# Slots and banks by one assignment, and a search that goes on from kept states, in a two-layer hybrid decoder trunk

## The chip, the cores and the metric

The kernel runs on one core of one Trainium2 chip. A core has TensorE (PE: matmuls into PSUM, a memory of eight banks), VectorE (DVE), ScalarE (ACT), GpSimd (POOL) and SyncE (SP), whose queue here issues every DMA transfer. The engines run side by side, each through its own list of instructions in the order in which they stand in it, and wait for one another on semaphores. The metric is the time of one launch in microseconds; shorter is better.

## The reference

Two layers over 1024 tokens of width 1024. Each layer normalizes, makes one projection, gives its columns to four token mixers, normalizes each mixer's output, projects back and adds; then comes a SwiGLU FFN of width 2816.

```python
for l in range(DEPTH):
    h = rmsnorm(x, attn_norm[l])
    proj = h @ w_in[l]
    (c_q, c_kv, k_r, g_b, g_c, u_conv, u_pool, q_sw, k_sw, v_sw) = jnp.split(proj, pts, axis=-1)
    y_a = mla_attention(...)        # 4 heads, causal, latent keys and values
    y_b = short_gated_conv(...)     # causal, width 3
    y_c = multiscale_pool(...)      # trailing means over 2, 4, 8, 16 tokens
    y_d = swa_sink_attention(...)   # window 128, grouped keys, ALiBi, sinks
    ...                             # RMSNorm of each group, then side by side as `mixed`
    x = x + mixed @ w_o[l]
    h2 = rmsnorm(x, ffn_norm[l])
    gate, up = jnp.split(h2 @ w_gate_up[l], 2, axis=-1)
    x = x + (jax.nn.silu(gate) * up) @ w_down[l]
return rmsnorm(x, final_norm)
```

## The kernel before

**The work.** Activations lie transposed, channels on the 128 partitions and tokens along the row, in two halves of 512 tokens. Every fp32 operand is split into a high part in the type fp32r (a copy that casts: line 301, or 223 for weights, on ScalarE) and the rest as a low part (a subtraction: line 304, or 224 for weights, on VectorE). A product is three fp32r matmuls: high by high, high by low, low by high (`mm3`, line 281). So TensorE cannot start on an operand before ScalarE has cast it, and cannot do its third matmul before VectorE has made the low part. In each layer the program first writes the projections and the four mixers (attention scores at lines 999 to 1001, transposes of probabilities at 1053, their products with the values at 1065), then the output projection, then the FFN, whose matmuls follow a scheme that forms seven products of sums of blocks (L1184 and L1186 make sums of the normalized input blocks, L1271 loads sums of weights that were made earlier and stored in DRAM under the name `gd`, L1459 is the SiLU on ScalarE, which needs a table load of its own, L1236 and L1238 load gate and up weights).

**Storage.** SBUF operands live in 47 slots of 128 x 2 x 512 floats, each one pair of halves (`Slots`; tiles are named u, then the slot, then a running number: `u33_4418` is tile 4418 in slot 33). PSUM tiles (ps_mm, ps_s, ps_t, ps_pv) get one of eight banks. A tile may be written once all readers of the slot's or bank's earlier tile are done; the semaphores for that follow from the choice of slot.

**The order.** No order is written by hand. `scheduled_kernel` traces the program once, builds a graph of the instructions with their dependencies and a cost for each (`Order`), and simulates the engines with ready lists (`_forward`), each engine taking the ready instruction with the lowest rank. In five rounds it gives banks (`Order.banks`) and slots (`Slots.place`, from the spans of `Order.spans`) by the planned begin and end of every tile, traces again, and runs a short search; the best round gets a long one (`_search`). A trial of the search changes ranks, either of instructions within a random stretch or along the chain that ends in one idle gap of TensorE, and replans the whole program; it is kept if the mean of four simulations with random lateness of the DMAs (`lates`) is lower. The order found is then imposed on each engine's list, SyncE's queue of DMAs included. In the numbers below, L281 of TensorE stands for all products, since the helper records their line.

Of the kernel before, what the change touches and what calls it, by code (L numbers as in the profile page):

```python
# [6 lines left out]

# [49 lines left out]
class Slots:  # L57

    def __init__(self, pool, n, spans=None):
        self.pool = pool
        self.spans = spans
        self.made = []
        self.until = [0.0] * n
        self.places = deque(range(n))
        self.halves = {F32: deque(), F32R: deque()}
        self.cur = [None] * n
        self.dt = [None] * n

    def place(self):

        if self.spans is None:
            return self.places.popleft()
        start, end = self.spans[len(self.made)]
        i = max(self.places, key=lambda i: u if (u := self.until[i]) <= start else -u)
        self.places.remove(i)
        self.until[i] = end
        return i

    def pair(self, dt):
        i = self.place()
        self.cur[i] = self.pool.tile([P, 2, HT], dt, name=f"u{i}", tag=f"u{i}", bufs=1)
        self.made.append(self.cur[i].name)
        self.dt[i] = dt
        return 2 * i
# [9 lines left out]
    def free(self, i):  # L96
        h = self.halves[self.dt[i // 2]]
        if i ^ 1 in h:
            h.remove(i ^ 1)
            self.places.append(i // 2)  # L100
        else:
            h.append(i)

    def free_pair(self, i):
        self.places.append(i // 2)
# [25 lines left out]
def trunk_kernel(ctx: ExitStack, tc: tile.TileContext, ins, out, given=None, spans=None, made=None):  # L131
# [10 lines left out]
    slots = Slots(ctx.enter_context(tc.tile_pool(name="slots", bufs=1)), N_U, spans)  # L142
    if made is not None:
        made.append(slots.made)
# [1663 lines left out]
TRIALS = 1500 if numba else 40  # L1808
# [42 lines left out]
def _forward(eng, kind, seen, taken, kb, want, late, hop, start, to, sync, count, rank, fixed, order):  # L1851

    n = eng.size
    left = count.copy()
    ready = np.zeros(n)
    end = np.zeros(n)
    begin = np.zeros(n)
    free = np.zeros(5)
    lk, lv = np.zeros((5, n)), np.zeros((5, n), np.int64)
    nk, nv = np.zeros((5, n)), np.zeros((5, n), np.int64)  # L1860
    ln, nn = np.zeros(5, np.int64), np.zeros(5, np.int64)
    done = np.zeros(5, np.int64)
    flying = np.zeros(LANES)
    issued = 0
    served = 0.0
    lock = 0.0
    table = 0
    for k in range(n):
        if left[k] == 0:
            e = eng[k]  # L1870
            _push(lk[e], lv[e], ln[e], 0.0, k)
            ln[e] += 1
    for _ in range(n):
        best, b = 1e18, -1
        for e in range(5):
            if fixed:
                if done[e] == 0:
                    pass
                i = done[e]
                k = order[e, i] if i < order.shape[1] else -1  # L1880
                if k < 0 or left[k] > 0:
                    continue
                t = max(free[e], ready[k])
            else:
                while ln[e] > 0 and lk[e, 0] <= free[e]:
                    k = lv[e, 0]
                    _drop(lk[e], lv[e], ln[e])
                    ln[e] -= 1
                    _push(nk[e], nv[e], nn[e], rank[k], k)
                    nn[e] += 1  # L1890
                if nn[e] > 0:
                    t = free[e]
                elif ln[e] > 0:
                    t = lk[e, 0]
                else:
                    continue
            if e == SP and issued >= LANES:
                t = max(t, flying[issued % LANES])
            if t < best:
                best, b = t, e  # L1900
        if b < 0:
            return end, begin, False
        t, e = best, b
        if fixed:
            k = order[e, done[e]]
        else:
            while ln[e] > 0 and lk[e, 0] <= t:
                k = lv[e, 0]
                _drop(lk[e], lv[e], ln[e])
                ln[e] -= 1  # L1910
                _push(nk[e], nv[e], nn[e], rank[k], k)
                nn[e] += 1
            k = nv[e, 0]
            _drop(nk[e], nv[e], nn[e])
            nn[e] -= 1
            order[e, done[e]] = k
        done[e] += 1
        more = 0.0
        if kind[k] >= TWO:
            get = max(t + 0.08, lock)  # L1920
            more = get - t - 0.08
            lock = get + max(0.05, seen[k] - (0.16 if kind[k] == TWO else 0.19))
        elif e == ACT and want[k] >= 0:
            if want[k] != table:
                more = 0.0 if kind[k] == TABLE else 1.29
                table = want[k]
        begin[k] = t
        free[e] = t + taken[k] + more
        end[k] = t + seen[k] + more
        if e == SP:  # L1930
            served = max(t + (1.31 if kind[k] == LOAD else 0.41), served) + kb[k] / 322.0
            end[k] = served + 0.82 + late[k]
            flying[issued % LANES] = end[k]
            issued += 1
        for i in range(start[k], start[k + 1]):
# [5 lines left out]
            if left[j] == 0 and not fixed:  # L1941
                _push(lk[eng[j]], lv[eng[j]], ln[eng[j]], ready[j], j)
                ln[eng[j]] += 1
    return end, begin, True
# [51 lines left out]
def _trials(arrays, graph, lates, order, limit):  # L1996

    eng, kind, seen, taken, kb, want, hop = arrays
    start, to, sync, count = graph[:4]
    none = np.zeros(0)  # L2000
    total = 0.0
    for s in range(lates.shape[0]):
        end, _, ok = _forward(
            eng, kind, seen, taken, kb, want, lates[s], hop, start, to, sync, count, none, True, order
        )
        if not ok:
            return 1e18
        total += end.max()
        if total + (lates.shape[0] - 1 - s) * (limit - 2.0) > lates.shape[0] * limit:
            return 1e18  # L2010
    return total / lates.shape[0]
# [3 lines left out]
def _search(arrays, graph, lates, margin, rank, trials, seed):  # L2015
# [5 lines left out]
    width = 0  # L2021
    for e in range(5):
        width = max(width, (eng == e).sum())
    order = -np.ones((5, width), np.int64)
    end, begin, _ = _forward(
        eng, kind, seen, taken, kb, want, margin, hop, start, to, sync, count, rank, False, order
    )
    best = _trials(arrays, graph, lates, order, 1e9)
    first = best
    wins = 0  # L2030
    rank = begin
    trial = -np.ones((5, width), np.int64)
    before = -np.ones(n, np.int64)
    for it in range(trials):
        new = rank.copy()
        if it % 2:
            lo = np.random.random() * end.max()
            hi = lo + math.exp(np.random.random() * 3.5 + 0.7)
            s = math.exp(np.random.random() * 4.0 - 1.5)
            some = np.random.randint(0, 10)  # L2040
            for k in range(n):
                if lo <= begin[k] < hi and (some >= 5 or eng[k] == some):
                    new[k] += s * np.random.randn()
        else:
            last = -1
            gaps = 0.0
            for q in range(width):
                k = order[PE, q]
                if k < 0:
                    break  # L2050
                if last >= 0:
                    gap = begin[k] - begin[last] - taken[last]
                    if gap > 0.04:
                        gaps += gap
                last = k
            pick = np.random.random() * gaps
            last, k = -1, -1
            for q in range(width):
                k = order[PE, q]
                if last >= 0:  # L2060
                    gap = begin[k] - begin[last] - taken[last]
                    if gap > 0.04:
                        pick -= gap
                        if pick <= 0:
                            break
                last = k
            for e in range(5):
                last = -1
                for q in range(width):
                    j = order[e, q]  # L2070
                    if j < 0:
                        break
                    before[j] = last
                    last = j
            s = math.exp(np.random.random() * 4.5 - 1.5)
            for _ in range(np.random.randint(3, 40)):
                new[k] -= s
                p, t = before[k], -1.0
                if p >= 0:
                    t = begin[p] + taken[p]  # L2080
                for i in range(bstart[k], bstart[k + 1]):
                    j = bto[i]
                    r = end[j] + hop[eng[k]] if bsync[i] else begin[j]
                    if r > t:
                        p, t = j, r
# [3 lines left out]
        e1, b1, _ = _forward(  # L2089
            eng, kind, seen, taken, kb, want, margin, hop, start, to, sync, count, new, False, trial  # L2090
        )
        if e1.max() > end.max() + 1.5:
            continue
        got = _trials(arrays, graph, lates, trial, best)
        if got < best:
            best = got
            rank, end, begin = b1, e1, b1
            order, trial = trial, order
# [384 lines left out]
```

## Time and profile before

| | |
|---|---|
| median of three runs | 2044.93 us (2044.12 to 2046.39) |
| the profiled execution | 2045.38 us |
| its span, first to last instruction | 2043.6 us |
| mean granted TensorE clock | 0.997 |
| TensorE without work in the span | 20.7 us (2043.6 - 2022.9) |
| DMA | 308.13 MB, mean 151 GB/s |

A row of the timeline gives the start, the length, the engine, the line, the operation, what it writes and reads, the shapes, how many were merged, and in brackets how long the engine had been idle and who ended that. A matmul's record of 512 columns lasts about 0.39 us, though the next one starts 0.227 us later; so starts, not lengths, tell the pace. A row by stretches gives for each engine the busy time and in brackets the number of instructions.

### The profile page before, as it was taken

How to read it: one execution, taken by the hardware profiler on the slowest of the kernel's cores; microseconds unless marked ns; L12 is line 12 of the kernel's file. 1: busy time of each engine (PE TensorE's matmuls, PEld its weight loads, DVE VectorE, ACT ScalarE, POOL GpSimd, SP SyncE). 2: the span in 40 equal slices, each digit the busy share in tenths (PEclk: the TensorE clock that was granted, in tenths of full speed). 3: DMA queues.
4: the chain of work that ended last, by engine and by line, in shares of the span. 5: the costliest groups of instructions: out<-in, count | busy, mean ns of one | idle time of the engine just before them, and what ended most of it. 6: DMA issues, size and time to landing. Idle time of an engine off the chain costs nothing. (4 is left out here: it accounts for less than half of the span.)

```text
span 2043.6 us, 26485 instructions
## 1 busy us (share of the span) xinstructions
PE 2022.9 (99%) x9398; PEld 1672.6 (82%) x9398; DVE 1578.5 (77%) x2553; ACT 998.8 (49%) x1753; POOL 438.9 (21%) x340
## 2 busy tenths in 40 slices
PE   9999999999999999999999999999999999999998
PEld 7888788878888888888888878888788888888887
DVE  8989979998677777655657999799977777776555
ACT  7458657743333334444434576577433333354342
POOL 0300000025565661000003000000356556500000
PEclk9999999999999999999999999999999999999999
DMA  6310223435555556766513112243455555487542
GB/s 244 127 44 21 84 63 110 149 128 179 179 177 183 176 188 246 259 211 222 176 38 128 56 27 78 65 134 119 145 191 186 177 173 191 169 296 235 195 161 98
DMA packets 144133, 308.13 MB, mean 151 GB/s; under 512 B 14080, under 2 KB 61184, under 8 KB 144000
## 3 DMA queue, kind: packets, MB, share of 16 engines
q1 hardware_dynamic: 144000, 306.43, 44.4%
q8 instruction: 74, 1.21, 0.2%
q14 instruction: 59, 0.48, 0.1%
HBM read 215.67 MB, written 89.65 MB: 149 GB/s over the span
## 5 line engine op out<-in xcount | busy, mean ns | idle before, releaser
L281 PE MATMUL ps_mm<-u,u 128*128 128x512 f32 (+1 forms) x3374 | 843.5, 390 | 7.0 <-ACT u L301 2.8
L281 PEld LDWEIGHTS ps_mm<-u,u 128*128 128x128 f32 x3374 | 615.4, 189 | 129.7 <-ACT u L301 3.6
L281 PE MATMUL ps_s<-u,u 128*128 128x512 f32 x2724 | 652.0, 389 | 0.2 <-DVE u L1214 0.2
L281 PEld LDWEIGHTS ps_s<-u,u 128*128 128x128 f32 x2724 | 510.9, 188 | 108.1 <-DVE u L1214 0.6
L301 ACT CAST u<-u 128x1024 fp32r<-128x1024 f32 (+2 forms) x426 | 361.8, 868 | 478.0 <-PE ps_s L281 116.3
L304 DVE TENSOR_TENSOR u<-u,u 128x1024 fp32r<-128x1024 f32 (+2 forms) x426 | 461.3, 1100 | 154.7 <-ACT u L301 107.0
L281 PE MATMUL ps_t<-u,u 128*128 128x512 f32 (+1 forms) x1092 | 251.9, 377 | 0.0
L281 PEld LDWEIGHTS ps_t<-u,u 128*128 128x128 f32 x1092 | 196.1, 188 | 39.1 <-DVE te L380 0.5
L281 PE MATMUL ps_pv<-u,u 128*128 128x512 f32 x696 | 167.4, 389 | 0.0
L281 PEld LDWEIGHTS ps_pv<-u,u 128*128 128x128 f32 x696 | 130.6, 188 | 27.3 <-DVE tp L1670 0.3
L1277 POOL TENSOR_TENSOR u<-u 128x512 f32<-128x512 f32 x38 | 73.3, 1928 | 226.9 <-DVE u L304 174.2
L1459 ACT ACTIVATE tp<-tp 128x512 f32<-128x512 f32 x76 | 48.0, 632 | 129.3 <-DVE tp L380 129.3
L1062 POOL MEMSET u<- 128x128 f32 x32 | 6.0, 214 | 471.9 <-PE ps_mm L281 250.9
L1247 POOL TENSOR_TENSOR u<-u,u 128x512 f32<-128x512 f32 x38 | 55.6, 1464 | 205.5 <-PE ps_s L281 109.2
L770 POOL TENSOR_TENSOR u<-u,u 128x512 f32<-128x512 f32 x6 | 8.0, 1337 | 413.1 <-ACT sm L628 326.4
L301 ACT CAST u<-ps_t 128x512 fp32r<-128x512 f32 (+3 forms) x132 | 64.8, 502 | 41.3 <-PE ps_t L643 16.6
L1539 POOL TENSOR_TENSOR u<-u 128x352 f32<-128x352 f32 x64 | 79.5, 1244 | 22.4 <-DMA u<-in_w_dn 18.7
L304 DVE TENSOR_TENSOR u<-ps_t,u 128x512 fp32r<-128x512 f32 (+3 forms) x132 | 75.2, 580 | 11.4 <-ACT u L301 10.7
L306 ACT ACTIVATE u<-u,par 128x512 fp32r<-128x512 f32 x92 | 64.6, 719 | 30.7 <-DVE u L380 10.3
L1461 DVE TENSOR_TENSOR tp<-tp,u 128x512 f32<-128x512 f32 x76 | 66.4, 873 | 16.3 <-ACT tp L1459 16.2
L345 ACT ACTIVATE tn<-u 128x512 f32<-128x512 f32 (+1 forms) x91 | 52.6, 597 | 52.2 <-DVE u L1723 45.4
L1249 POOL TENSOR_TENSOR u<-u,u 128x512 f32<-128x512 f32 x38 | 71.8, 1890 | 1.6
(199 smaller groups left out, 2383.5 us busy)
## 6 DMA issues: line engine op xcount, KB each, us to landing
u<-in_w_gu SPq DMA_DIRECT2D x94, 512.0 KB, 4.0
ad<-u SPq DMA_DIRECT2D x154, 256.0 KB, 2.1
u<-ad SPq DMA_DIRECT2D x70, 512.0 KB, 6.0
u<-in_w_dn SPq DMA_DIRECT2D x64, 352.0 KB, 3.3
qd<-u SPq DMA_DIRECT2D x64, 352.0 KB, 2.8
u<-qd SPq DMA_DIRECT2D x32, 512.0 KB, 5.2
u<-in_w_in SPq DMA_DIRECT2D x28, 512.0 KB, 3.9
u<-in_w_dn SPq DMA_DIRECT2D x24, 512.0 KB, 6.5
```

What stands on the lines that cost most here:

```text
L281: pe.matmul(o, w, r, start=start and k == 0 and i == 0, stop=stop and k == n - 1 and i == 2, skip_group_check=again,)
L301: a = act.copy(hi, f)
L304: dve.tensor_tensor(out=lo, in0=f, in1=rd(hi), op=ALU.subtract)
L306: a = act.activation(hi, f, AF.Copy, scale=gain)
L345: act.activation(q, f, AF.Square)
L770: pool.tensor_tensor(out=F.ap(q + 1), in0=a21, in1=a22, op=ALU.add)
L1247: pool.tensor_tensor(out=F.ap(q + 1), in0=a21, in1=a22, op=ALU.add)
L1249: pool.tensor_tensor(out=a21, in0=F.ap(q + 1), in1=a11, op=ALU.add)
L1277: pool.tensor_tensor(out=q4, in0=q4, in1=F.ap(self.raw[1] + 1), op=ALU.add)
L1459: last_silu = act.activation(g, g, AF.Silu)
L1461: dve.tensor_tensor(out=g, in0=g, in1=r, op=ALU.mult)
L1539: pool.tensor_tensor(out=o, in0=a, in1=b, op=ALU.add)
```

## The change

It replaces three pieces of the planner; no instruction of the trunk is added or removed.

- Slots and banks. Before, a tile took, in the program's order, the place that had been free for the shortest time at its planned start (or, with none free, the one that gets free first). Now all tiles are chained at once by a linear assignment over the whole plan: following one tile by another in the same place costs 1/(gap + 0.5) for a planned gap, and 10 and more for an overlap.
- The search. It keeps the state of the simulation at 60 moments of the accepted plan. A trial begins from the last kept state ahead of its change, runs to 60 us behind the changed stretch, and is dropped there if TensorE has then not worked at least 0.02 us more than in the accepted plan. There are 40000 trials instead of 1500, and both kinds of trial now pick their place by a gap of TensorE.
- The four simulations that judge a trial now also shake ACT, DVE and POOL instructions, by an exponential of mean 0.03 us less that mean.

```diff
     def place(self):
-        if self.spans is None:
+        if self.homes is None:
             return self.places.popleft()
-        start, end = self.spans[len(self.made)]
-        i = max(self.places, key=lambda i: u if (u := self.until[i]) <= start else -u)
+        i = self.homes[len(self.made)]
         self.places.remove(i)
-        self.until[i] = end
         return i
...
-TRIALS = 1500 if numba else 40
+TRIALS = 40000 if numba else 40
+STOPS, HORIZON = 60, 60.0
...
+@compiled
+def _worked(arrays, s, t):
+
+    taken, begin, order, m = arrays[3], s[3], s[8], s[6][10]
+    w = 0.0
+    for i in range(m):
+        k = order[PE, i]
+        if begin[k] >= t:
+            break
+        w += min(taken[k], t - begin[k])
+    return w
...
-            lo = np.random.random() * end.max()
-            hi = lo + math.exp(np.random.random() * 3.5 + 0.7)
...
+        k = at[min(m - 1, np.searchsorted(gaps[:m], np.random.random() * total))]
+        new = rank.copy()
+        hi = s[3][k]
+        lo = hi
+        if it % 2:
+            lo = max(0.0, hi - math.exp(np.random.random() * 4.0))
+            hi = lo + math.exp(np.random.random() * 3.5 + 0.7)
...
+        _copy(marks[max(0, min(STOPS - 1, int((lo - 1.0) / step)))], work)
...
+        stop = hi + HORIZON
+        _run(arrays, graph, margin, new, False, stop, work)
+        if _worked(arrays, work, stop) < _worked(arrays, s, stop) + 0.02:
             continue
-        got = _trials(arrays, graph, lates, trial, best)
+        _run(arrays, graph, margin, new, False, 1e18, work)
+        if work[2].max() > s[2].max() + 1.5:
+            continue
+        got = _trials(arrays, graph, lates, work[8], best)
...
-        self.lates = np.stack([moves * draw.exponential(0.5, self.n) for _ in range(4)])
+        others = np.array([e in ("Activation", "DVE", "Pool") for e in self.engine])
+        self.width = max(self.engine.count(e) for e in self.ENGINES)
+        self.lates = np.stack(
+            [
+                draw.exponential(moves * 0.5 + others * 0.03, self.n) - others * 0.03
+                for _ in range(4)
+            ]
+        )
...
+    @staticmethod
+    def chains(start, over, born, gone, places):
+
+        n = len(start)
+        gap = start[None, :] - over[:, None]
+        cost = np.where(gap > 0, 1.0 / (np.maximum(gap, 0) + 0.5), 10.0 - 10.0 * np.minimum(gap, 0))
+        cost[gone[:, None] >= born[None, :]] = 1e7
+        full = np.zeros((n + places, n + places))
+        full[:n, :n] = cost
+        after = [int(k) for k in linear_sum_assignment(full)[1]]
+        home, i = [None] * n, 0
+        for k in sorted(set(range(n)).difference(after[:n])):
+            while k < n:
+                home[k] = i
+                k = after[k]
+            i += 1
+        return home
...
     def banks(self, begin, end):
...
-            b = max(range(8), key=lambda b: free[b] if free[b] <= start else -free[b])
-            free[b] = max(end[k] for k in self.users[m])
-            given.append(b)
-        return given
...
+        return self.chains(start, over, born, gone, 8)
```

What it does to the lists is shown at three places. The new program's line numbers are higher by 4 for the trunk (L301 is L305). Names have the slot's number after u.

ScalarE at the entry to the FFN of layer 0. `_4420` is the high part of the first FFN weights, cast from `_4418`; the rows on `tp_` cast sums of input blocks; `_4158` is a gate block that SiLU works on. Before:

```order
L301 CAST u43_4327<-u22_4321 128x512
L301 CAST u14_4385<-tp_4379 128x512
L301 CAST u25_4391<-tp_4388 128x512
L301 CAST u44_4395<-tp_4389 128x512
L1459 ACT_TABLE_LOAD
L1459 ACTIVATE u1_4158<-u1_4158 128x512
L301 CAST u5_4420<-u33_4418 128x1024
L301 CAST u31_4405<-tp_4399 128x512
```

And in the new program:

```order
L305 CAST u13_4395<-tp_4389 128x512
L305 CAST u22_4420<-u24_4418 128x1024
L305 CAST u3_4401<-tp_4398 128x512
L305 CAST u16_4426<-u10_4424 128x1024
L305 CAST u41_4411<-tp_4408 128x512
L305 CAST u34_4405<-tp_4399 128x512
L376 ACTIVATE tn_4237<-tn_4236 128x512
L305 CAST u37_4415<-tp_4409 128x512
L1324 COPY u43_3845<-ps_mm_4436 128x512
L305 CAST u29_4432<-u24_4430 128x1024
L1463 ACT_TABLE_LOAD
L1463 ACTIVATE u40_4158<-u40_4158 128x512
```

The table load and the first SiLU stood ahead of the cast of `_4420`, and now stand nine rows and more behind it.

TensorE in the mixers of layer 0, where the projection weights `_2113` are first used: `_2115` is their high part, `_2116` the low one, `ps_mm_2171` and `ps_mm_2196` the products, `ps_s_21..` attention scores. Before:

```order
L999 MATMUL ps_s_2133<-u0_1846,u43_2060 128x256
L1000 MATMUL ps_s_2133<-u0_1846,u43_2060 128x256
L1001 MATMUL ps_s_2133<-u0_1846,u43_2060 128x256
L281 MATMUL ps_mm_2196<-u22_298,u33_2115 128x512
L281 MATMUL ps_mm_2171<-u15_156,u33_2115 128x512 x2
L281 MATMUL ps_mm_2171<-u15_156,u14_2116 128x512
L281 MATMUL ps_mm_2171<-u16_166,u33_2115 128x512 x2
L999 MATMUL ps_s_2163<-u0_1846,u43_2060 128x512
L1000 MATMUL ps_s_2163<-u0_1846,u43_2060 128x512
L1001 MATMUL ps_s_2163<-u0_1846,u43_2060 128x512
```

And now:

```order
L285 MATMUL ps_mm_2171<-u15_156,u9_2115 128x512 x2
L285 MATMUL ps_mm_2196<-u26_298,u9_2115 128x512 x2
L285 MATMUL ps_s_2239<-u2_1504,vhi_2235 128x512 x2
L285 MATMUL ps_s_2239<-u2_1504,vlo_2236 128x512
L285 MATMUL ps_s_2239<-u44_1645,vhi_2235 128x512
L285 MATMUL ps_mm_2258<-vhi_2253,u25_1796 128x256
L285 MATMUL ps_mm_2258<-vlo_2254,u25_1796 128x256
L285 MATMUL ps_mm_2258<-vhi_2253,u25_1796 128x256 x2
L285 MATMUL ps_mm_2258<-vlo_2254,u25_1796 128x256
L285 MATMUL ps_mm_2258<-vhi_2253,u25_1796 128x256
L285 MATMUL ps_s_2239<-u44_1645,vhi_2235 128x512
L285 MATMUL ps_s_2239<-u44_1645,vlo_2236 128x512
```

The first read of `_2116` followed two matmuls behind the first of `ps_mm_2171`; now it stands behind these rows and three more matmuls of 256 columns (`ps_mm_2270`), and the three of `ps_s_2163` stand ahead of the first row.

SyncE's queue at the entry to the FFN of layer 1; `_13155` is the first weight sum that it needs. Before:

```order
L1218 DMA xr_87<-u15_7423 128x512
L1282 DMA u9_12956<-gd1_1_9797 128x512
L1282 DMA u9_12956<-gd1_2_9809 128x512
L1236 DMA u24_13261<-in_w_gu 128x1024
L1271 DMA u26_13155<-gd1_0_9785 128x1024
L1271 DMA u34_13161<-gd1_1_9797 128x1024
L1271 DMA u13_13167<-gd1_2_9809 128x1024
```

And now:

```order
L1222 DMA xr_87<-u22_7423 128x512
L1286 DMA u29_12956<-gd1_1_9797 128x512
L1286 DMA u29_12956<-gd1_2_9809 128x512
L1275 DMA u37_13155<-gd1_0_9785 128x1024
L1275 DMA u3_13161<-gd1_1_9797 128x1024
L1275 DMA u22_13167<-gd1_2_9809 128x1024
L1240 DMA u3_13261<-in_w_gu 128x1024
```

The load of `in_w_gu` moved behind the three weight sums, and `_13155` has another slot: slot 26's earlier tile is last read by the L1184 that makes `tp_13125`, slot 37's by the one that makes `tp_13115`, two VectorE instructions earlier.

More of the change, by code (lines that the diff above doesn't have):

```diff
@@ L1935, in _forward @@
+            floats[5] = max(t + (1.31 if kind[k] == LOAD else 0.41), floats[5]) + kb[k] / 322.0
+            end[k] = floats[5] + 0.82 + late[k]
+            floats[7 + ints[15] % LANES] = end[k]
+            ints[15] += 1
+        else:
+            floats[e] = t + taken[k] + more
+            end[k] = t + seen[k] + more
         for i in range(start[k], start[k + 1]):
@@ L2020, in _search @@
     np.random.seed(seed)
[L2021 to L2032, printed above, removed]
+    s = _forward(arrays, graph, margin, rank, width)
+    best = _trials(arrays, graph, lates, s[8], 1e9)
@@ L2033, in _search @@
+    first, rank, wins, stale = best, s[3].copy(), 0, True
+    marks = [_blank(eng, count, width) for _ in range(STOPS)]
+    work = _blank(eng, count, width)
     before = -np.ones(n, np.int64)
+    gaps, at = np.zeros(width), np.zeros(width, np.int64)
     for it in range(trials):
-        new = rank.copy()
-        if it % 2:
-            lo = np.random.random() * end.max()
-            hi = lo + math.exp(np.random.random() * 3.5 + 0.7)
[L2039 to L2048, printed above, removed]
+        if stale:
+            stale = False
+            for e in range(5):
+                for q in range(width):
+                    j = s[8][e, q]
+                    if j < 0:
+                        break
+                    before[j] = s[8][e, q - 1] if q else -1
+            m, total = 0, 0.0
+            for q in range(1, width):
+                k, p = s[8][PE, q], s[8][PE, q - 1]
@@ L2067, in _search @@
[L2067 to L2075, printed above, removed]
+                gap = s[3][k] - s[3][p] - taken[p]
+                if gap > 0.04:
+                    total += gap
+                    gaps[m], at[m] = total, k
+                    m += 1
@@ L2317, in scheduled_kernel, with trace @@
 def scheduled_kernel(fresh, ins_of, rounds=5, trials=TRIALS):
[L2321 removed]
+    def trace(banks, homes=None, order=None):
         nc = fresh()
```

289 lines of the change are left out of this document (157 added, 132 removed).

## The prediction

> **What bounds the kernel.** I read the page's busy line first, then the busy time by stage, then the waits of TensorE, then the timeline at the longest of them.
>
> ```profile
> span 2043.6 us, 26485 instructions
> PE 2022.9 (99%) x9398; PEld 1672.6 (82%) x9398; DVE 1578.5 (77%) x2553; ACT 998.8 (49%) x1753; POOL 438.9 (21%) x340
> ```
>
> TensorE shows 20.7 us without work. That is not all it loses, because a matmul's record is longer than its turn. The stages tell more (first and last microsecond, length, then busy time and count of each engine, granted clock, DMA share, GB/s):
>
> ```profile
> 6.50:430.00 423.50, 417.67 (x2010) 342.06 (x2011) 383.13 (x806) 277.57 (x583) 19.63 (x28) 0.99 0.30 102
> 430.00:1010.00 580.00, 580.00 (x2559) 479.77 (x2559) 411.50 (x468) 229.61 (x307) 200.42 (x140) 1.00 0.58 197
> 1010.00:1440.00 430.00, 426.21 (x2064) 349.70 (x2063) 365.12 (x775) 259.34 (x547) 19.50 (x28) 1.00 0.26 87
> 1440.00:2034.60 594.60, 594.01 (x2744) 496.72 (x2744) 413.19 (x489) 227.87 (x311) 199.19 (x140) 1.00 0.55 186
> ```
>
> The second row is the FFN of layer 0, with 512-column matmuls alone: 580.00/2559 = 0.227 us from start to start, without a hole. There nothing can be won by order. The first and third rows are the mixers. Their narrower matmuls go at these paces:
>
> ```profile
> 239.02 0.49 PE L1053 MATMUL ps_t<-cst,u 128*128 128x128 f32 x3
> 240.05 0.34 PE L999 MATMUL ps_s<-u,u 128*128 128x384 f32 x1
> 240.58 0.28 PE L999 MATMUL ps_s<-u,u 128*128 128x256 f32 x1
> 240.70 0.28 PE L1000 MATMUL ps_s<-u,u 128*128 128x256 f32 x1
> ```
>
> So 0.18 us for 384 columns (three from 240.05 to 240.58), 0.12 for 256 (the last two starts), and 0.11 for 128 (0.49 us for three, less a record of about 0.27, halved). By the program's shapes the first mixer stage has 1530, 40, 220 and 220 matmuls of 512, 384, 256 and 128 columns: 346.9 + 7.2 + 26.4 + 24.2 = 404.7 us, so 18.8 of its 423.5 us are lost. The other has 1582, 40, 220 and 220: 416.4 us, so 13.6 of 430.0 are lost. The change can win at most these 32.4 us; the 9.0 us from 2034.6 to the span's end are a chain of final normalization and stores that stands in the same order in both programs, and the start differs by one small load.
>
> **The change, part by part.** It adds and removes no work: by kind, each engine has the same instructions before and after. It gives other slots and banks and another order, so what it is worth is the waits that it takes away, less those that it makes. Six places lose most.
>
> Place 1, the entry to the FFN of layer 0 (TensorE, ScalarE, SyncE):
>
> ```profile
> 415.60 0.69 DVE L1184 TENSOR_TENSOR tp<-u,u 128x512 f32<-128x512 f32 x1
> 416.35 0.32 SPq L1271 DMA_DIRECT2D u<-gd  x1
> 420.04 1.28 ACT L1459 ACT_TABLE_LOAD   x1
> 421.33 0.63 ACT L1459 ACTIVATE u<-u 128x512 f32<-128x512 f32 x1
> 421.87 1.03 ACT L301 CAST u<-u 128x1024 fp32r<-128x1024 f32 x1
> 420.65 0.61 PE L281 MATMUL ps_s<-u,u 128*128 128x512 f32 x2
> 422.95 0.74 PE L281 MATMUL ps_mm<-u,u 128*128 128x512 f32 x2 [1.68 <-ACT u L301]
> 423.53 0.63 PE L281 MATMUL ps_s<-u,u 128*128 128x512 f32 x2
> 424.22 4.14 PE L281 MATMUL ps_mm<-u,u 128*128 128x512 f32 x10
> 428.20 0.63 PE L281 MATMUL ps_s<-u,u 128*128 128x512 f32 x2
> u<-gd SPq DMA_DIRECT2D x6, 512.0 KB, 4.0
> ```
>
> TensorE waits for the cast of the weights, which waits behind a table load and a SiLU pass of 1.28 + 0.63 us on ScalarE. The start before the wait is 420.65 + 0.61 - 0.39 = 420.87, so 422.95 - 420.87 - 0.23 = 1.85 us are lost. Then come slow matmuls: ten in 428.20 - 424.22 = 3.98 us instead of 2.27, and four in 1.27 instead of 0.91. In all 1.85 + 1.71 + 0.36 = 3.9 us. The new order puts the table load behind the cast. The next limit is the load: issued at 416.35, landed 4.0 later at 420.35, cast until 421.4, where TensorE comes at 421.27. I keep 0.3 us of wait and win 3.6. The delayed SiLU passes are needed only by the gate blocks later; nothing of TensorE waits for them here.
>
> The slow stretch goes with the wait:
>
> ```profile
> 207.00:210.00 3.00, 1.13 (x3) 0.68 (x4) 3.00 (x7) 1.18 (x3) 0.00 (x0) 0.88 0.09 31
> 210.00:213.00 3.00, 3.00 (x9) 2.30 (x8) 3.00 (x9) 2.16 (x5) 0.00 (x0) 0.55 0.53 164
> 423.00:428.00 5.00, 4.94 (x14) 3.58 (x15) 5.00 (x9) 3.02 (x5) 0.00 (x0) 0.66 0.31 105
> ```
>
> The granted clock falls to 0.55 and 0.66 after the two waits of more than 1.6 us, and returns to 1.00. [...] The trace has it after 1.68 and 1.87 us, so I go by the trace. [...]
>
> Place 2, layer 0, the first projection with new weights:
>
> ```profile
> 206.36 1.26 PE L281 MATMUL ps_mm<-u,u 128*128 128x512 f32 x3
> 208.21 1.22 DVE L224 TENSOR_TENSOR u<-u,u 128x1024 fp32r<-128x1024 f32 x1
> 209.49 1.65 PE L281 MATMUL ps_mm<-u,u 128*128 128x512 f32 x3 [1.87 <-DVE u L224]
> 210.93 0.63 PE L999 MATMUL ps_s<-u,u 128*128 128x512 f32 x1
> 212.21 1.53 PE L281 MATMUL ps_mm<-u,u 128*128 128x512 f32 x5
> ```
>
> TensorE reads the low half of the split (L224) two matmuls after the first read of the high half, and VectorE makes it late. From 206.36 to the last start of the last row (212.21 + 1.53 - 0.39 = 213.35) pass 6.99 us for 13 matmuls, 2.95 by pace: 4.0 lost. The new order puts three more 512-column score matmuls ahead of the stretch, and before the first read of the low half fifteen that stood elsewhere, six of 512 and nine of 256 columns: 0.68 + 1.36 + 1.08 = 3.1 us of cover for 1.87 + 0.16 = 2.0 us of wait. I win 4.0; if VectorE comes to L224 later by all that was moved, nothing.
>
> Place 3, the entry to the FFN of layer 1:
>
> ```profile
> 1424.99 0.68 DVE L1184 TENSOR_TENSOR tp<-u 128x512 f32<-128x512 f32 x1
> 1425.74 0.33 SPq L1236 DMA_DIRECT2D u<-in_w_gu  x1
> 1427.09 0.32 SPq L1271 DMA_DIRECT2D u<-gd  x1
> 1432.57 1.05 ACT L301 CAST u<-u 128x1024 fp32r<-128x1024 f32 x1 [1.33 <-DMA u<-gd]
> 1433.67 0.74 PE L281 MATMUL ps_mm<-u,u 128*128 128x512 f32 x2 [1.11 <-ACT u L301]
> ```
>
> A wait shown as 1.11 costs 1.11 + 0.16 (a record of 0.39 hides 0.16 beyond the pace), and some 0.3 more in the next four starts: 1.6. The load came 5.5 us before the cast, behind another half megabyte from L1236. Now that load stands behind, and the slot is one whose last reader is the L1184 of 1424.99: issued by 1425.8, landed by 1429.8. I win all 1.6.
>
> Places 4 to 6:
>
> ```profile
> 242.33 0.50 PE L999 MATMUL ps_s<-u,u 128*128 128x512 f32 x1 [0.67 <-ACT u L1018]
> 245.26 0.73 PE L281 MATMUL ps_mm<-u,u 128*128 128x512 f32 x2 [0.37 <-DVE u L307]
> 1221.33 0.50 PE L999 MATMUL ps_s<-u,u 128*128 128x512 f32 x1 [0.55 <-ACT u L1021]
> 1222.92 0.96 PE L281 MATMUL ps_mm<-u,u 128*128 128x512 f32 x3 [0.62 <-DVE u L224]
> 1253.80 0.30 PE L1053 MATMUL ps_t<-cst,u 128*128 128x128 f32 x1 [0.82 <-DVE u L1037]
> ```
>
> With 0.16 on each: 1.36, 1.49 and 0.98 us. In the new order other matmuls stand ahead of four of the five waiting ones (not of 1221.33); I win 3.0 of 3.8.
>
> The six hold 3.9 + 4.0 + 1.6 + 3.8 = 13.3 us and give 12.2. The other 19 us of loss are spread over many short waits, no row of which says which go: between none and two thirds (12.7). I take 4, a fifth, since the waits of under 0.16 us look like the pipeline's own. New waits: between none and rival B's; I take three of the size of place 6, 1 us each. Sum: 12.2 + 4 - 3 = 13.2. Against the profiled execution's 2045.4 us this is 2032; the median of the runs, 2044.9, lies 0.5 lower, which I leave inside the range.
>
> **Rivals.** A: no change that can be told. VectorE is the real limit of the mixers: 383.13 of 423.50 us, and it is busy without a hole from 207 to 213 and 423 to 428. If its order cannot feed TensorE sooner, the waits come back a few matmuls later, at 2041 to 2049. Against it: at place 1 ScalarE, at place 3 a DMA was late, and 404.7 us leave VectorE room.
>
> B: slower, by late loads. The new order issues weights nearer to their use: the projection weights of place 2 stand in row 50 of SyncE's queue instead of row 30, the output weights after them in row 54 instead of 31.
>
> ```profile
> u<-in_w_in SPq DMA_DIRECT2D x28, 512.0 KB, 3.9
> ```
>
> A load that is issued only when it is needed costs 3.9 us and a slow stretch like place 1's (2.1): 6.0. It turns the result to slower by over 0.2% (4.1 us, about what a measurement of this kernel can tell from no change) when three loads are that late: 13.2 - 18.0, that is 2050. For it: one queue serves all, in order. Against it: the loads still stand behind earlier matmuls by tens of rows.
>
> [...]
>
> D: nearly all short waits go too: 13.3 + 12.7 = 26, that is 2019.
>
> **Chances.** The forecast (2024 to 2040) 0.62, C 0.10, D 0.08, A 0.13, B 0.07. Faster: 0.62 + 0.10 + 0.08 = 0.80; same 0.13; slower 0.07. The range 2021 to 2043 leaves out most of B, half of A and some of D, 0.18.
>
> **What would show it.** No wait of TensorE over 1.6 us after the start, and the granted clock at 1.00 in every stretch between; the table load behind the cast at the FFN's entry; mixer stages of about 415 and 424 us and FFN stages at 580 and 595 as before. If FFN stages grow, B is right. If the mixers are as long with waits at other lines, A is right. The prediction fails if the chip's waits were never those that the plan's costs see.

## The result, and the profile after

The changed kernel takes 2028.72 us (median of four runs, 2027.98 to 2029.33) beside 2045.12 for the kernel before in the same session: a ratio of 0.9919, 95% interval 0.9902 to 0.9936. That is 16.4 us faster (16.7 by the two profiled spans); 13.2 were forecast.

The page's first lines, of the changed kernel:

```profile
span 2026.9 us, 26551 instructions
PE 2014.8 (99%) x9398; PEld 1673.7 (83%) x9398; DVE 1573.5 (78%) x2553; ACT 1000.8 (49%) x1753; POOL 447.9 (22%) x340
```

The number of matmuls is the same, and TensorE is without work for 12.1 us instead of 20.7. The stages, cut at the same moments as before (length, busy time and count of each engine, granted clock, DMA share, GB/s):

```profile
6.50:430.00 423.50, 422.44 (x2053) 348.38 (x2052) 386.73 (x817) 280.81 (x586) 21.03 (x28) 1.00 0.31 105
430.00:1010.00 580.00, 579.85 (x2557) 479.50 (x2556) 414.32 (x469) 237.20 (x314) 206.24 (x140) 1.00 0.59 198
1010.00:1440.00 430.00, 429.40 (x2098) 357.45 (x2097) 367.35 (x784) 258.98 (x548) 26.54 (x31) 1.00 0.25 84
1440.00:2017.90 577.90, 577.31 (x2672) 482.96 (x2670) 398.83 (x469) 219.45 (x299) 193.85 (x137) 1.00 0.56 191
```

By 1440 us the changed kernel has started 6708 matmuls in the first three rows, against 6633 before: 75 more, and 75 x 0.227 = 17.0 us is the whole gain, within the rounding of such a count. In the FFN of layer 0 the pace is the same (580.00 us for 2557 matmuls, 2559 before). TensorE's longest waits are now these (engine, tile, line, who ended it: total, times, longest):

```profile
PE ps_pv L501 <- DVE ones L159: 1.1, 1, 1.1
PE ps_s L372 <- ACT tn L371: 0.6, 1, 0.6
PE ps_t L365 <- DVE u L308: 0.6, 2, 0.3
PE ps_s L1003 <- ACT u L305: 0.4, 1, 0.4
PE ps_mm L285 <- ACT tn L1361: 0.2, 1, 0.2
```

The first is the start of the program. The entry to the FFN of layer 0, place 1 of the prediction, reads now (timeline; four lines were added, so L301 is L305 and L1459 is L1463):

```profile
413.68 1.05 ACT L305 CAST u<-u 128x1024 fp32r<-128x1024 f32 x1 [1.49 <-DVE tp L1188]
...
415.07 0.62 PE L285 MATMUL ps_mm<-u,u 128*128 128x512 f32 x2
...
421.64 1.28 ACT L1463 ACT_TABLE_LOAD   x1
```

The cast ends at 414.73 and TensorE reads it at 415.07 without a wait; the table load starts 6.9 us behind the cast's end, and the granted clock is 1.00 from 413 to 422 us.

For the loss as a whole I took from each matmul's start to the next one's start the pace of its width (the paces of the prediction) and summed what is over. Before: 32.6 us, of which 18.9 in the first mixer stage and 13.7 in the second. After: 15.8, of which 9.7 and 6.1.

### The profile page after: what moved, and what is told of

Read it like the earlier page. It is cut to its first block, busy times and chain, and to the rows that moved or that the text cites. A ratio compares the mean times of both kernels' runs of the same rounds, so it can differ in the third digit from the quotient of the medians.

```text
span 2026.9 us, 26551 instructions
## 1 busy us (share of the span) xinstructions
PE 2014.8 (99%) x9398; PEld 1673.7 (83%) x9398; DVE 1573.5 (78%) x2553; ACT 1000.8 (49%) x1753; POOL 447.9 (22%) x340
## 4 chain that ended last, share of the span: by engine, by line
PE 71%; DVE 5%; ACT 1%; issue 0%; DMA 0%; DVEq 0%; ACTq 0%; SPq 0%
PE ps_s L285 26%; PE ps_mm L285 23%; PE ps_t L285 10%; PE ps_pv L285 8%; DVE u L308 1%; PE ps_pv L1069 1%; PE ps_t L1057 1%; DVE u L311 0%; PE ps_s L1004 0%; PE ps_s L1005 0%; PE ps_s L1003 0%; DVE u L357 0%; DVE u L384 0%; PE ps_pv L659 0%; DVE u L1218 0%
## 5 line engine op out<-in xcount | busy, mean ns | idle before, releaser
L285 PE MATMUL ps_mm<-u,u 128*128 128x512 f32 (+1 forms) x3374 | 822.5, 389 | 0.5 <-ACT tn L1361 0.2
L285 PE MATMUL ps_s<-u,u 128*128 128x512 f32 x2724 | 644.5, 389 | 0.0
L305 ACT CAST u<-u 128x1024 fp32r<-128x1024 f32 (+2 forms) x426 | 362.2, 868 | 451.2 <-PE ps_s L285 91.3
L1463 ACT ACTIVATE tp<-tp 128x512 f32<-128x512 f32 x76 | 48.1, 632 | 159.4 <-DVE tp L384 159.3
L1251 POOL TENSOR_TENSOR u<-u,u 128x512 f32<-128x512 f32 x38 | 61.5, 1620 | 226.9 <-DMA u<-in_w_gu 91.7
L1281 POOL TENSOR_TENSOR u<-u 128x512 f32<-128x512 f32 x38 | 61.2, 1612 | 210.2 <-DVE u L308 207.8
L774 POOL TENSOR_TENSOR u<-u,u 128x512 f32<-128x512 f32 x6 | 9.3, 1552 | 367.3 <-PE ps_pv L659 287.5
L1543 POOL TENSOR_TENSOR u<-u 128x352 f32<-128x352 f32 x64 | 83.7, 1310 | 12.2 <-DMA u<-in_w_dn 10.4
L305 ACT CAST u<-ps_t 128x512 fp32r<-128x512 f32 (+3 forms) x132 | 64.0, 506 | 40.6 <-PE ps_t L647 24.6
L384 DVE TENSOR_TENSOR tp<-tp,u 128x512 f32<-128x512 f32 x76 | 78.2, 1029 | 1.6
L1543 POOL TENSOR_TENSOR u<-u,u 128x352 f32<-128x352 f32 x64 | 71.1, 1111 | 4.2
```

Source lines behind the costliest of these rows:

```text
L285: pe.matmul(o, w, r, start=start and k == 0 and i == 0, stop=stop and k == n - 1 and i == 2, skip_group_check=again,)
L305: a = act.copy(hi, f)
L384: dve.tensor_tensor(out=o, in0=a, in1=b, op=ALU.mult)
L1251: pool.tensor_tensor(out=F.ap(q + 1), in0=a21, in1=a22, op=ALU.add)
L1281: pool.tensor_tensor(out=q4, in0=q4, in1=F.ap(self.raw[1] + 1), op=ALU.add)
L1463: last_silu = act.activation(g, g, AF.Silu)
```

## Experiments

### Which part of the change: places or search

First the old rule for places with the new search:

```diff
-        i = self.homes[len(self.made)]
+        start, end = self.homes[len(self.made)]
+        i = max(self.places, key=lambda i: u if (u := self.until[i]) <= start else -u)
 ...   # and the old loop in Order.banks
```

> The changed kernel, with slots and banks given one by one as before (each buffer takes the free place whose last use ends latest); the new search with 40000 trials stays. Theory S (the longer, cheaper search finds an order with fewer waits, whatever the places are): 2029 to 2034 us, TensorE's longest wait after the start under 1.6 us. Theory P (the assignment gives the gain, because buffers no longer wait for the last readers of their places): 2038 to 2045, with waits of 1 us and more at TensorE behind writes into places that were read late. My own guess is between, nearer to S: 2033.

Then the new places with the old search of 1500 trials (the kernel before, with `Slots`, `chains`, `banks` and `homes` of the changed one):

> The kernel before, with slots and banks from the assignment; the old search of 1500 trials and its lateness for transfers alone stay. Theory S: 2038 to 2045, the waits of the kernel before at other lines. Theory P: 2028 to 2034, since the places alone take the waits away. If the two parts add up, the gain here and the loss of the run with the old places make 16.4 us together; if they need each other, less here and more there. My guess: 2038.

| places | old search | new search |
|---|---|---|
| old | 2046.44 us | 2042.16, ratio 0.998 (0.997 to 0.9989) |
| assigned | 2028.92, ratio 0.9917 (0.9902 to 0.9932) | 2028.72 |

Theory P is right and my guesses were wrong: the assignment gives 17.5 us with the old search, and the new search adds 0.2 to that by the medians and nothing by the ratios (0.9917 and 0.9919). The search alone is worth 4.3 us, and only with the old places. The changed kernel's 2028.72 is from the first session, where the kernel before took 2045.12; in the later ones it took 2046.44 to 2046.64. So differences to 2028.72 below are about 1 us larger than the ratios give.

With the old places the long search still leaves a wait at place 2 (timeline, then the granted clock behind it; line numbers are higher by 7 here, L231 makes the low half, and L314 is the last reader of its slot):

```profile
207.29 0.75 DVE L314 SCALAR_TENSOR_TENSOR u<-u,par,u 128x512 fp32r<-128x512 f32 x1
...
207.95 0.68 DVE L387 TENSOR_TENSOR te<-ps_mm,u 128x512 f32<-128x512 f32 x1
208.55 1.22 DVE L231 TENSOR_TENSOR u<-u,u 128x1024 fp32r<-128x1024 f32 x1
208.69 0.73 PE L288 MATMUL ps_mm<-u,u 128*128 128x512 f32 x2 [1.19 <-DVE te L387]
...
209.82 0.62 PE L288 MATMUL ps_mm<-u,u 128*128 128x512 f32 x1 [0.40 <-DVE u L231]
```

```profile
210.00:213.00 3.00, 3.00 (x8) 0.51 0.39 130
```

The wait of 1.19 is one for a bank: `ps_mm_2171` goes into the bank of `ps_mm_2088`, which L387 reads until 208.63 (207.95 + 0.68), and TensorE starts 0.06 us later. In the changed kernel the bank of `ps_mm_2171` had been empty for 9.2 us.

With the assigned places and the old search, 1500 trials are enough to leave only these (waits of TensorE; the first is at 7.4 us, at the start):

```profile
PE ps_s L285 <- ACT u L305: 1.1, 1, 1.1
PE ps_pv L501 <- DVE ones L159: 1.1, 1, 1.1
PE ps_s L372 <- ACT tn L371: 0.6, 1, 0.6
PE ps_t L1057 <- ACT u L1022: 0.6, 1, 0.6
```

Two smaller parts of the search, each undone in the changed kernel:

```diff
-                draw.exponential(moves * 0.5 + others * 0.03, self.n) - others * 0.03
+                moves * draw.exponential(0.5, self.n)
```

> The changed kernel, but the four drawn plans in which an order is judged make only transfers late, as before, and not the instructions of ScalarE, VectorE and GpSimd (mean 0.03 us). Theory S and theory P both say that this part does little: 2026 to 2032. Theory J (an order that keeps small reserves against late vector work is what the short waits needed, since those of 5 to 100 ns make about half of what TensorE loses): 2033 to 2040, with more of the waits under 0.2 us and hardly more of the longer ones.

```diff
-TRIALS = 40000 if numba else 40
+TRIALS = 1500 if numba else 40
```

> The changed kernel with 1500 trials in place of 40000 (150 in place of 4000 in each of the first five rounds). Theory S, in the form that the number of trials does it: 2036 to 2043, near the kernel before. Theory P: 2028 to 2032, since the places are still the assigned ones. That trials continue from kept states changes only what a trial costs to work out, not what the chip does, so it shows here only through the number of trials. My guess: 2036.

Measured 2029.07 us (ratio 0.9919, 0.9903 to 0.9936) and 2030.61 (0.9925, 0.991 to 0.994). The lateness of vector work does nothing that can be told, so theory J falls. Cutting the trials to a 27th costs 1.9 us by the medians and 1.2 by the ratios.

Each of these programs is one plan, and no run shows how far two plans of one rule differ when only chance in the search does. A difference of 1 to 3 us between two plans is therefore not put down to a cause here. The assignment's own effect is larger: the five programs with assigned slots and banks and their preference take 2028.7 to 2031.5 us (this section's, and one more below), and those with the old rule, or with only one of the assignment and the preference, 2042 to 2052.

### Slots or banks

> The changed kernel with the SBUF slots given as before (the free slot whose last use ends latest) and the PSUM banks from the assignment. The run with both given as before took 2042.2 us and the changed kernel 2028.7, so 13.4 us lie between. Theory SL (the slots hold the gain: at the longest waits of the old places the late write goes to a slot whose last reader is late, as the low half of a split at 208 us and the loaded weights at 1431 us): 2037 to 2043, and the wait at 208 us with its slow matmuls is back. Theory BA (the banks hold it: a TensorE write that waits for VectorE to read a bank): 2029 to 2033.

> The changed kernel with the PSUM banks given as before and the SBUF slots from the assignment. Theory SL: 2029 to 2034, no wait at 208 us. Theory BA: 2037 to 2043. If the two parts add up, this run and the one with the old slots lose 13.4 us together.

Measured 2037.19 us (0.9955, 0.994 to 0.997) with the old slots, 2037.72 (0.9957, 0.9942 to 0.9972) with the old banks. Neither theory is right alone: each costs 8.5 to 9 us, and both together 13.4, so they overlap (by the ratios 7.4, 7.8 and 12.5). Of the two waits that theory SL named, the old slots brought back the one at the FFN entry of layer 1 (1.53 us at 1423.98, the second row of the first fence), but not the one at 208 us; it is the old banks that did (at 209.32, the first row of the second fence; 1.22 us by starts, that is from one matmul's start to the next less the pace), with a mean granted clock of 0.998 in the profiled run, as in the changed kernel. With the old slots TensorE waits mostly here:

```profile
PE ps_t L650 <- DVE tp L639: 3.4, 4, 1.7
PE ps_mm L288 <- ACT u L308: 1.5, 1, 1.5
```

and with the old banks in more and shorter pieces:

```profile
PE ps_mm L285 <- DVE u L228: 1.1, 1, 1.1
...
PE ps_t L647 <- DVE tp L636: 0.9, 1, 0.9
PE ps_mm L285 <- DVE te L384: 0.9, 1, 0.9
PE ps_s L1003 <- ACT u L1022: 0.7, 1, 0.7
```

### Why the assignment: room, or no conflicts

The assignment differs from the old rule in two ways: it looks at the whole plan, and it prefers a place that has been empty for long, where the old rule takes the one that came free last. One word changed in each rule of the kernel before parts the two from one side:

```diff
-        i = max(self.places, key=lambda i: u if (u := self.until[i]) <= start else -u)
+        i = min(self.places, key=lambda i: self.until[i])
...
-            b = max(range(8), key=lambda b: free[b] if free[b] <= start else -free[b])
+            b = min(range(8), key=lambda b: free[b])
```

> The kernel before with one word changed in each of its two rules: a new buffer takes the place that has been free longest, in place of the one that came free last. No assignment, the old search. Theory G (what counts is the slack between the last read and the next write of a place): 2029 to 2034, near the run with the assigned places and the old search (2028.9). Theory W (it takes an assignment over the whole plan, since a rule that gives one after another leaves some buffers a place that is read late): 2036 to 2044.

and the assignment with its preference turned round, from the other:

```diff
-        cost = np.where(gap > 0, 1.0 / (np.maximum(gap, 0) + 0.5), 10.0 - ...)
+        cost = np.where(gap > 0, 2.0 - 2.0 / (np.maximum(gap, 0) + 1.0), 10.0 - ...)
```

> The changed kernel, still with an assignment over the whole plan and still with a high cost on a place that is read late, but with the preference turned round: among the places that are free in time, the cost now grows with the time that a place stays empty (2 - 2/(gap + 1) in place of 1/(gap + 0.5)). Theory R (room: the assignment wins because it leaves time between the last read and the next write; before, 150 of 510 banks in the mixers were written again less than 0.5 us after their last read, in the changed kernel 58 of 512): 2038 to 2044, with as many tight banks as before. Theory N (no conflicts: it wins because, over the whole plan, hardly any buffer gets a place that is read after its own time; the run with the longest-free places, 2052, had room as well, 79 of 509 under 0.5 us, and was slower): 2028 to 2033.

Measured: longest free 2052.13 us, slower than before (1.0027, 1.0016 to 1.0038); assignment with tight places 2045.07, the same as before (0.9992, 0.9982 to 1.0001). From the traces I counted, for each bank and slot in the two mixer stages, how often the next tile is first touched less than 0.5 us after the last instruction on the tile before it:

| kernel | time, us | banks under 0.5 us | slots under 0.5 us |
|---|---|---|---|
| before | 2045 | 150 of 510 | 185 of 604 |
| old places, new search | 2042 | 132 of 510 | 183 of 601 |
| assigned, tight | 2045 | 140 of 509 | 189 of 603 |
| old slots | 2037 | 48 of 512 | 202 of 603 |
| old banks | 2038 | 168 of 511 | 167 of 601 |
| assigned places, old search | 2029 | 44 of 512 | 167 of 602 |
| changed | 2029 | 58 of 512 | 166 of 604 |
| longest free, one by one | 2052 | 79 of 509 | 135 of 595 |

The first seven rows say that the time roughly follows the room: an assignment without the preference for room is worth nothing (theory N falls; theory R's range ended 1 us lower), and one with it 13 to 18 us. The last row says that room, so counted, is not enough: the rule that takes places one by one has about half as many tight banks as before, the fewest tight slots, and is the slowest. So theory G falls. Theory W's direction holds, that the preference without the assignment wins nothing, but its range (2036 to 2044) missed, and its reason, that some buffers get a place that is read late, is not shown. What the longest-free rule does wrong stays open; its waits are others:

```profile
PE ps_t L643 <- DVE tp L632: 2.8, 4, 0.9
PE ps_pv L655 <- ACT u L301: 2.2, 3, 1.3
PE ps_pv L655 <- DVE u L304: 1.8, 3, 0.8
```

One more version took the places from the searched order again in each round (`found` in place of `plan.find()`), in the hope of beating both kernels:

> The changed kernel, but from the second of its five rounds on the places are assigned by the times of the order that the round before has found, and the search goes on from that order, in place of the times of the first, unsearched plan. If the places limit what the search can find: 2022 to 2027. If what is left (15.8 us of pace lost at TensorE, the longest wait after the start 0.56) is no longer due to the places: 2027 to 2031, the same as the changed kernel. I expect the second, at 2028.

It took 2031.48 us (0.9925, 0.991 to 0.9939), 2.8 us more than the changed kernel by the medians and 1.2 by the ratios. The first reading falls, the second missed by 0.5 us, and nothing here beats the changed kernel.

### Place 1 by itself

The kernel before, with the first SiLU pass and its table load behind the casts of the weights:

```diff
+    first = row.pop(at("Activation", "_4158"))
+    row.insert(at("Copy", "_4432") + 1, first)
```

> The kernel before, with nothing else changed but ScalarE's row at place 1: the first SiLU pass, and with it the table load, behind the casts of the weights (as in the changed kernel). By the prediction's working of place 1 the wait of 1.68 at 423 us shrinks to at most 0.3 and the ten slow matmuls behind it go at full pace, since they follow from the wait: 3.6 us less, 2041.3 beside 2044.9. Rival C (the slow matmuls belong to something else): the wait goes, the granted clock around 425 us stays near 0.66, and 1.6 us are won. Rival L (the place, not the order: the cast waits then for its transfer into a slot that came free late): a wait of 0.7 us or more stays at the same matmul, now behind a DMA, and under 2.5 us are won.

It won nothing: 2046.31 us beside 2046.64, ratio 0.9998 (0.9989 to 1.0008). The timeline (this run is 0.6 us behind the kernel before as it comes here), then the stretches behind it:

```profile
421.07 0.68 DVE L1184 TENSOR_TENSOR tp<-u,u 128x512 f32<-128x512 f32 x1
...
421.79 1.04 ACT L301 CAST u<-u 128x1024 fp32r<-128x1024 f32 x1 [1.19 <-DVE tp L1184]
...
422.88 0.73 PE L281 MATMUL ps_mm<-u,u 128*128 128x512 f32 x2 [1.03 <-ACT u L301]
422.93 0.69 DVE L1184 TENSOR_TENSOR tp<-u,u 128x512 f32<-128x512 f32 x1
...
423.54 1.22 DVE L304 TENSOR_TENSOR u<-u,u 128x1024 fp32r<-128x1024 f32 x1
...
424.81 1.54 PE L281 MATMUL ps_mm<-u,u 128*128 128x512 f32 x3 [0.73 <-DVE u L304]
```

```profile
423.00:426.00 3.00, 2.27 (x7) 0.83 0.36 120
426.00:429.00 3.00, 3.00 (x9) 0.61 0.15 55
```

The cast does not wait for its data. It writes tile 4420 into slot 5, and the L1184 at 421.07 is the last reader of tile 4298 in that slot: the cast starts 0.04 us after it ends. In the kernel before that reader stands here,

```profile
420.47 0.69 DVE L1184 TENSOR_TENSOR tp<-u,u 128x512 f32<-128x512 f32 x1
```

so it ended at 421.16, and the cast, which began at 421.87, could have begun 0.7 us earlier at most. TensorE comes 0.7 us earlier, relative to the rest, and gives it back four matmuls later, where it waits for the low half (L304), which VectorE makes at the same relative time as before. By starts, the wait of 1.84 has become 1.20 + 0.90, and the slow matmuls are there as before (granted clock 0.83 and 0.61 in the two rows above, 0.66 from 423 to 428 us before). Rival L comes nearest, with VectorE in the place of the DMA.

### What a wait costs in clock

Two programs that ran once each, the changed kernel with ScalarE's row rearranged at the same FFN entry:

```diff
+    late = row.pop(at("Copy", "_4420"))      # cast_late_2, with _4426 behind it
+    row[at("Copy", "_4405") + 1 ...] = [late, other]
...
+    late = row.pop(at("Copy", "_4426"))      # cast_late_3
+    row.insert(at("Activation", "tn_4237") + 1, late)
```

> The changed kernel with ScalarE's row at the FFN entry of layer 0 rearranged: the two casts of weight blocks stand behind three casts of activations, so that TensorE waits at 415 us. By the rows of the changed kernel the first of them ends some 2.4 us later and had 0.3 of reserve: a wait of about 2.1 us. Theory K (waits of about 1.9 us in a short stretch make the granted clock fall for a few us): eight or more matmuls at 0.43 in place of 0.227 us follow, granted clock near 0.6, and 4 us are lost in all. [...]

> The changed kernel with the second of the two weight casts behind the square of the norm that waits for VectorE: it starts about 418.6 in place of 415.15, so TensorE waits some 3.4 us at 416 us. Theory K: the granted clock falls for a few us, as many slow matmuls as after the waits of 1.9 us in the kernel before, 5 us lost. [...]

The first took 2031.51 us, the second 2034.83. The wait of the first, and the granted clock behind it:

```profile
417.87 0.73 PE L285 MATMUL ps_mm<-u,u 128*128 128x512 f32 x2 [1.84 <-ACT u L305]
```

```profile
417.00:420.00 3.00, 2.13 (x9) 1.00 0.00 0
420.00:423.00 3.00, 3.00 (x15) 1.00 0.53 175
```

and of the second:

```profile
419.55 1.22 PE L285 MATMUL ps_mm<-u,u 128*128 128x512 f32 x2 [3.41 <-ACT u L305]
```

```profile
420.00:423.00 3.00, 3.00 (x8) 0.50 0.01 4
423.00:426.00 3.00, 3.00 (x9) 0.61 0.00 0
```

Theory K falls as a rule of length: 2.00 us without a start (row: 1.84) left the clock at 1.00, though behind the 1.85 at place 1 of the kernel before it was 0.50 from 424.34 to 427.75 us. After a wait of 3.58 us by starts (row: 3.41), twelve matmuls went at 0.43 us in place of 0.227.

## Why the prediction was right, and where not

The sign, the stages and the size came out, and the time lies in the range. The cause given for the largest terms did not, or only in part, so that the number is in part luck.

- **What bounds the kernel.** Right: all of the gain is TensorE's waits in the mixer stages and at their ends, the FFN stages have the same pace, and of the 32.6 us lost in the mixers about half (16.8) could be won. Rival A's reason, that VectorE is the limit, is refuted for the sum: 386.73 us of VectorE's work fit beside 9.7 us of loss. It is right for one spot: at place 1 VectorE's low half sets the time (the 0.73 at 424.81, above).
- **The six places: 12.2 expected, 12.8 measured** (of 13.3 there remain 0.27 at 416.25 and 0.23 at 1418.31; no step of over 0.15 us is left at place 2 nor at places 4 to 6). But the step "the new order puts the table load behind the cast" fails as a cause: that move, alone, won nothing, where I had written that I win 3.6. That nearly all of place 1's loss went nevertheless is luck in the sum. And the prediction read the waits as work that stands late in a wrong order, where the trace of before had more to say. At places 4 and 5 the first matmul does not wait for an operand; it writes a bank that ScalarE's L1018 or L1021 has read until 0.14 us before (242.33 less 241.50 + 0.69):

```profile
241.50 0.69 ACT L1018 ACTIVATE u<-ps_s,sm 128x512 f32<-128x512 f32 x1 [1.47 <-DVE sm L1007]
```

  In the changed kernel the same two tiles get banks that have been empty for 0.7 and 7.9 us, and no wait for a bank is left there; the order around them changed too, and no run parts the two. The other waits of places 4 to 6 name instructions that make an operand (at place 6 the bank had been free for 0.6 us). At places 1 to 3 the new place did not take the wait away directly. In both kernels tile 4420 follows tile 4298 into its slot, 2116 follows 503, and 13157 (place 3) follows 13035; the cast of place 1 waits for the last reader of its slot in the changed kernel too (the 1.49 at 413.68, above), only 1.4 us before TensorE needs it. At place 2 the order did what the prediction said: VectorE ends the low half at 210.24, later than before (209.43), and TensorE, busy with the matmuls that were to cover it, reads it at 210.46 without a wait. The run with the old search shows that the assigned places suffice for these three waits to go; which of the other places let the order be found, or VectorE and ScalarE be early at places 1 and 3, no run shows.
- **The rest and the new waits** were mis-sized. New steps of over 0.3 us are four (200.69, 223.36, 473.18, 1196.79: 0.48 + 0.56 + 0.32 + 0.44 = 1.8 us) where 3 were taken. The spread waits gave 16.7 - 12.8 + 1.8 = 5.7 where 4 were taken. Together that is 2.9 of the 3.5 us by which the sum was short; the six places hold the other 0.6. The shortest steps, which the prediction took for the pipeline's own, stayed: steps of 5 to 20 ns held 6.1 us in the mixers before and hold 5.6 now, while those of over 100 ns fell from 22.6 (88 of them) to 7.7 (47). What makes the shortest is not shown.
- **Rival B** did not come: no TensorE wait on a weight load is among the waits above. **Rival C**, that the slow matmuls do not come from the waits and stay (2036 us), did not come either, and no run shows a ground for its chance of 0.10: the slow stretches went with their waits (in the changed kernel the granted clock is 1.00 from 207 to 213 and from 413 to 422 us), and came back with one (the second of the last two runs, 0.50 from 420 to 423 us).
- **What no term or rival asked** was which of the three parts does it. The prediction spoke of the order throughout. With the old places the new search won 4.3 us, at 2042; the rest of the gain is the places'.

## What to carry to other kernels

When a wait is put down to an instruction that makes none of the waiting one's inputs, look for what that instruction reads: it may be the last reader of the slot or bank to be written. A planner that gives out buffers is worth trying with a preference for places that have been empty for long, by one assignment over the whole plan: here that won 17.5 us with 1500 trials of search, where 40000 trials with the old rule for places won 4.3. The preference alone, one buffer after another, lost 5.5, and the assignment without it won nothing. Moving one instruction at the longest wait is worth trying alone before the wait's whole length is counted as a gain.

## What the runs showed of the hardware

In these runs the length of a wait between 1.8 and 2.0 us did not by itself tell the granted clock behind it. The clock was halved after waits that summed to 1.84 us (place 1 before; 0.50 from 424.34 us) or 1.92 (place 2 with the old places, 1.35 + 0.57; 0.51 from 210 to 213 us), and stayed at 1.00 after a single 2.00 (the first of the two runs above, from 414 to 426 us). What decides it is not shown.

The clock's own record in the trace of the kernel before holds only 1.00 and 0.50 (0.55 or 0.66 are means over stretches that hold both). Ahead of the end of the program it is 0.50 twice. The stretch ahead of the first and the first itself, then the second (length, busy time and count of TensorE, granted clock, DMA share, GB/s):

```profile
205.89:209.30 3.41, 1.59 (x8) 1.00 0.15 38
209.30:212.71 3.41, 3.22 (x8) 0.50 0.39 117
```

```profile
424.34:427.75 3.41, 3.41 (x9) 0.50 0.40 137
```

In the halved stretch from 209.30 us, matmuls of 512 columns start 0.427 us apart in place of 0.227 (three steps from 210.93 to 212.21). Eight of them fill 3.41 us and lose some 1.6 us (an estimate from these paces), so that a wait of 1.9 us costs about 3.5 where the clock is halved behind it, and 1.9 where it is not.
